# The last norm on three engines, the last convolution's sums in PSUM, and two reordered steps in a two-layer decoder trunk

## The chip, the cores and the metric

The kernel runs on one core of a Trainium2 chip. The metric is the device time of one execution in microseconds. Before the change it is 2335.38 us, the median of 3 runs (2333.52 to 2335.58).

## The reference

A residual stream x of 1024 tokens and 1024 features goes through two layers and a last RMSNorm. All is float32.

```python
for l in range(2):
    h = rmsnorm(x, g_mix[l])
    mem_k, mem_v = split(rmsnorm(mem, g_mem) @ w_mem_kv[l])
    if l == 0:                                # layer A
        p = h @ w_in_a                        # [GLU input 2*768 | memory queries 256]
        v = a * sigmoid(gate)                 # a, gate: the halves of the GLU input
        mix = silu(layernorm(causal_dwconv(v, width 31)))
    else:                                     # layer B
        kvf = rmsnorm(x, g_kv) @ w_kvf        # K, V (12 heads of 64) and 12 forget logits
        cum_logf = cumsum(log_sigmoid(f_logit + b_f))
        q, q_mem = split(h @ w_in_b)
        mix = causal softmax(q k / 8 + cum_logf[t] - cum_logf[s]) @ v
    x = x + concat(mix, memory_attention(q_mem, mem_k, mem_v)) @ w_out[l]
    x = x + conv_ffn(rmsnorm(x, g_ffn[l]))    # up to 2*2816, width-3 conv, silu(gate)*val, down
return rmsnorm(x, g_final)
```

## The kernel before

The stream is kept transposed, features on the 128 partitions and tokens along the free axis: `x[k]` is one of 8 tiles of 128x1024. A float32 product is made of three products of rounded halves (`mm3`, lines 108 to 110): each operand is split into a high and a low part (`split`, lines 81 and 82: ScalarE casts, GpSimd or VectorE subtracts). Tokens are handled in halves of 512 (`hf`).

A planner sets the order on each engine: it takes the instructions in the order in which the code issues them as priorities, estimates when each is ready and how long it takes, and writes one fixed order for each engine, with the semaphores. A tile that takes a slot (its `tag`) waits until the tile before it in that slot has been used for the last time. Three things push the order by hand. `later(100)` lowers the priority of what is issued in it. `issue_after(ins)` puts what it issues behind `ins`, on the engine of `ins` alone. `set_fill` takes a list of small steps, and each `mark` of a matrix product issues the next few of them, so that PE has products to do while an attention waits on other engines; `drain_fill(n)` issues the next n at once.

PSUM has the slots c0 to c3 (128x512 each) and b2a, b2b (128x1024 each). Tiles that ask for "b1" take c0 to c3, or what `ring` names, in turn.

Layer A. Each of the six channel tiles t gets its gate and value products (`ug`, `ua`, in c0 and c1), and then the convolution of 31 taps, split over three engines: PE (`tap`, sums in `cpe`, a b2 slot), GpSimd (ScalarE multiplies into `ct`, GpSimd adds to `yp`, line 875), and VectorE. For t under 5, VectorE adds its taps in place in the PSUM tile `cpe` (line 918). For the last, t = 5, it keeps a sum of its own, `ca`, one 128x512 tile a half, for 10 taps (lines 886 and 888), adds it to `yp` (889), and `rest` adds PE's part and writes `v` (914). PE's taps of t = 5 go half by half. Between these stand the memory attention's steps (scores `ms` in c2, weights `amp`, transposes `mt` in c3, outputs `mo` in c2). Then `lnorm(hf)` sums the six `v` over the channels into `mean`, a tile in c0 for the first half and c1 for the second (line 1014), beside the fill of `mem_step` products (`om`).

Layer B. `normed` puts its sums `st` and broadcasts `bc` in c2 and c3 in turn. `memattn(0)` makes the memory queries `pq` in c0 and c1, and runs the memory attention, with scores in b2 and `mt`, `mo` in c2, c3; its marks issue the V steps. `v_steps(pc_)` makes, for a third of the heads, eight tiles `vps` (one for each 128 tokens, 24 products in four steps), in c0 and c1 in turn; ScalarE and VectorE evict each (lines 1128 to 1131). Then K and Q of the first pair of heads are made (`kq_steps(0)`, 32 steps: K first half, K second half, Q first half, Q second half, 8 steps each; evicted by lines 1181 and 1183). The forget logits become log sigmoids, are transposed (`lft`) and summed along the tokens by one scan on VectorE, `cum` (line 1215). Its high and low parts and their negatives are written to `d_c` and read back as rows of the operands `q2` and `k2` by `prep` (lines 1241 and 1242); the scores of the forgetting attention (1260, 1261, 1263) need them in their second product. Before `prep`, `drain_fill(AHEAD)` with AHEAD = 20 issues 20 steps of the second pair's K and Q; their products take c0, so each half waits until the half before it has been evicted.

The end. `down_final` makes the last down-projection in quarters i of 256 tokens. For each feature tile m: three times three products, VectorE adds to x (662), ScalarE squares (693), GpSimd or, late, VectorE sums the squares (696). Then a square root, a reciprocal (142) and a broadcast row in PSUM, `rows[i]` (123), and `scale(i, k)` multiplies x[k] by `g_final` and the row on VectorE (683) and stores it from SP's queue (685). Those products run FLAG = 15 steps behind; the last fifteen of the 32 come after everything else on VectorE, behind `add2`.

Of the kernel before, what the change touches and what calls it, by code (L numbers as in the profile page):

```python
# [8 lines left out]
F32 = mybir.dt.float32  # L9
F32R = mybir.dt.float32r  # L10
BF16 = mybir.dt.bfloat16
AF = mybir.ActivationFunctionType
ALU = mybir.AluOpType
AX = mybir.AxisListType

P = 128
S = 1024
HS = 512
# [12 lines left out]
VP = 260  # L31
# [20 lines left out]
class Trunk:  # L52
# [363 lines left out]
    def ffn(self, l):  # L416
        nc, tc = self.nc, self.tc
# [214 lines left out]
        with tc.tile_pool(name=f"dn{l}", bufs=1) as fp:  # L632
            self.ps.n, self.ps.ring = 0, ("c0", "c1", "c2", "c3", "b2a", "b2b")
            gs = {}
            G, N0 = 4, 3

            def prep(c):
                w = self.load_w(self.wdn[l, c], [D], name=f"wd{l}",
                                pools=None if c < N0 else ((fp, "dh", 7), (fp, "dl", 7)))
                g = self.main.tile([P, S], F32, tag="raw", name="g", bufs=self.NRAW)  # L640
                nc.sync.dma_start(g, self.d_g[c])
                hs = []
                for hf in range(2):
                    hi, lo = self.htile("gh"), self.htile("gl")
                    self.split(hi, lo, g[:, hf * HS:(hf + 1) * HS])
                    hs.append((hi, lo))
                gs[c] = (hs, w)

            def add_x(k, hf):
                xs = self.nt("xs")  # L650
                sl = slice(hf * HS, (hf + 1) * HS)
                nc.sync.dma_start(xs, self.d_x[:, k, sl])
                nc.vector.tensor_tensor(self.x[k][:, sl], self.x[k][:, sl], xs, op=ALU.add)

            def down_part(ts, m, hf, q=slice(0, HS), first=False):
                ps = self.ps.tile([P, HS], F32, tag="b1", name="dn")[:, :q.stop - q.start]
                self.mm3(ps, [(wh[:, m * P:(m + 1) * P], wl[:, m * P:(m + 1) * P], hs[hf][0][:, q], hs[hf][1][:, q])
                              for hs, (wh, wl) in ts])
                sl = slice(hf * HS + q.start, hf * HS + q.stop)
                if first:  # L660
                    return nc.scalar.copy(self.x[m][:, sl], ps)
                return nc.vector.tensor_tensor(self.x[m][:, sl], self.x[m][:, sl], ps, op=ALU.add)  # L662


            def down(cs):
                ts = [gs.pop(c) for c in cs]
                for hf in range(2):
                    for m in range(KD):
                        down_part(ts, m, hf, first=cs[0] == 0)
                        if cs[0] == N0:  # L670
                            add_x(m, hf)

            def down_final(cs):

                ts = [gs.pop(c) for c in cs]
                Q = 2 * P
                accs = fp.tile([P, 4, Q], F32, tag="y", name="facc", bufs=2)
                sqs = fp.tile([P, 4, Q], F32, tag="y", name="fsq", bufs=2)
                rows, queue = {}, []

                def scale(i, k):
                    sl = slice(i * Q, (i + 1) * Q)
                    nc.vector.scalar_tensor_tensor(self.x[k][:, sl], self.x[k][:, sl], self.vec("g_final", k), rows[i],
                                                   op0=ALU.mult, op1=ALU.mult)
                    nc.sync.dma_start(self.out[:, k, sl], self.x[k][:, sl])

                for i in range(4):
                    sl = slice(i * Q, (i + 1) * Q)
                    acc = accs[:, i]
                    for m in range(KD):  # L690
                        add = down_part(ts, m, i // 2, slice(i % 2 * Q, (i % 2 + 1) * Q))
                        sq = acc if m == 0 else sqs[:, m % 4]
                        nc.scalar.activation(sq, self.x[m][:, sl], AF.Square)
                        if m > 0:
                            e = nc.vector if i == 3 and m >= self.FDVE else nc.gpsimd
                            add2 = e.tensor_tensor(acc, acc, sq, op=ALU.add)
                        g = 8 * i + m - self.FLAG
                        if g >= 0 and g // KD < i:
                            with self.issue_after(add.ins):
                                scale(g // KD, g % KD)  # L700
                            queue.remove((g // KD, g % KD))
                    tmp = self.ps.tile([P, 2, HS], F32, tag="b2", name="fin")
                    r = self.rstd_cols(acc, 2, D, self.eps_rms, tmp[:, 1, :2])
                    rows[i] = self.bcast_row(r, 2, tmp[:, 0, :Q])
                    queue += [(i, k) for k in range(KD)]
                with self.issue_after(add2.ins):
                    for q in queue:
                        scale(*q)

            cs = [list(range(0, N0))] + [list(range(c, min(c + G, NF))) for c in range(N0, NF, G)]  # L710
            for c in cs[0]:
                prep(c)
            self.x = [unit(f"x{k}") for k in range(KD)]
            for i, c in enumerate(cs):
                for c2 in cs[i + 1] if i + 1 < len(cs) else ():
                    prep(c2)
                if i + 1 == len(cs):
                    self.ps.n, self.ps.ring = 0, ("c0", "c1", "c2", "c3")
                (down if l == 0 or i + 1 < len(cs) else down_final)(c)

    def layer_a(self):
        nc, tc = self.nc, self.tc
# [130 lines left out]
        def conv_steps(t):  # L853
# [6 lines left out]
            d = {}  # L860


            def start():
                d["vh"] = pb.tile([P, CW - 1 + S], F32R, tag="vh", name="vh")
                d["vl"] = pb.tile([P, CW - 1 + S], F32R, tag="vl", name="vl")
                self.split(d["vh"], d["vl"], v, lo_eng=nc.vector)
                with self.later(self.LATER):
                    y = d["y"] = pb.tile([P, 2, HS], F32, tag="yp", name="yp", bufs=2)
                    for hf in range(2):
                        nc.scalar.activation(y[:, hf], v[:, hf * HS + ne:hf * HS + ne + HS], AF.Identity,  # L870
                                             bias=self.vec("b_dwa", t), scale=w(ne))
                        for j in range(ne + 1, np_):
                            c = pb.tile([P, HS], F32, tag="ct", name="ct", bufs=2)
                            nc.scalar.activation(c, v[:, hf * HS + j:hf * HS + j + HS], AF.Copy, scale=w(j))  # L874
                            nc.gpsimd.tensor_tensor(y[:, hf], y[:, hf], c, op=ALU.add)  # L875
                if last:

                    with self.later(self.LATER):
                        d["a"] = []
                        for hf in range(2):  # L880
                            a = self.nt("ca")
                            d["a"].append(a)
                            for j in range(np_, CW):
                                vj = v[:, hf * HS + j:hf * HS + j + HS]
                                if j == np_:
                                    nc.vector.tensor_scalar(a, vj, w(j), None, op0=ALU.mult)
                                else:
                                    nc.vector.scalar_tensor_tensor(a, vj, w(j), a, op0=ALU.mult, op1=ALU.add)
                            nc.vector.tensor_tensor(y[:, hf], y[:, hf], a, op=ALU.add)
# [155 lines left out]
    def layer_b(self):  # L1045
# [60 lines left out]
        def v_steps(pc_):  # L1106
# [3 lines left out]
            def step(i):  # L1110
# [2 lines left out]
                if i == 0:  # L1113
                    load_v(pc_ + 1)
                if kk == 0:
                    d["ps"] = self.ps.tile([P, VP], F32, tag=f"c{t % 2}", name="vps")
                ps = d["ps"]
                tsl = slice(ti * P, (ti + 1) * P)
                for k in (2 * kk, 2 * kk + 1):
# [45 lines left out]
        def kq_steps(t):  # L1165
# [3 lines left out]
            def step(i):  # L1169
# [8 lines left out]
                proj_half(d["w" + n], d["u"], hf, [k])  # L1178
                if k == KD - 1:
                    if n == "k":  # L1180
                        nc.vector.tensor_tensor(d[n][:, sl], d["u"], rb[:, sl], op=ALU.mult)
                    else:
                        nc.vector.scalar_tensor_tensor(d[n][:, sl], d["u"], SCALE, rb[:, sl],
                                                       op0=ALU.mult, op1=ALU.mult)
# [27 lines left out]
        on = unit([NFOX, S], F32, "on")  # L1212
        nc.gpsimd.memset(on, 1.0)
        cum = unit([NFOX, S], F32, "cum")
        nc.vector.tensor_tensor_scan(cum, on, lf, 0.0, op0=ALU.mult, op1=ALU.add)
        ch = unit([NFOX, S], F32R, "ch")
        cl = unit([NFOX, S], F32R, "cl")
        nc.scalar.copy(ch, cum)
# [86 lines left out]
                    nc.tensor.matmul(po, lhsT=vs[:, j], rhs=pl[:, u], start=False, stop=j == 2 * I + 1)  # L1305
            self.fold_rows(o, po, e, self.nt("fr", 2 * P))

        self.drain_fill(self.AHEAD)
        vss = {(0, 0): prep(0, 0), (0, 1): prep(0, 1)}
        its = [(t, e, I) for t in range(CT) for e in range(2) for I in range(4)]  # L1310
        pend = []
# [268 lines left out]
```

## Time and profile before

| | |
|---|---|
| median of 3 runs | 2335.38 us (2333.52 to 2335.58) |
| the profiled execution | 2334.59 us |
| its span | 2332.8 us |
| mean granted TensorE clock | 0.988 |
| PE busy | 2256.2 us, 97% |
| VectorE (DVE) busy | 1460.0 us, 63% |
| GpSimd (POOL) busy | 1333.7 us, 57% |
| ScalarE (ACT) busy | 1075.5 us, 46% |
| DMA | 216.74 MB, mean 93 GB/s |

The profile is of one execution on the chip. "PEld" is TensorE's weight load, which overlaps PE's products; "SPq" is the queue from which DMAs are issued. Rows in time give start and length in us, engine, line, operation, output and inputs, shape, how many were merged (x), and in brackets the engine's idle time before and what ended it. Rows of groups give, behind the count, busy us and mean ns of one, then idle us before. Rows of the waits give the total, the number and the longest, in us.

### The profile page before, as it was taken

The page shows a single profiled execution, that of the slowest core. Times are in us where ns is not written, and L with a number is a line of the kernel's source. Part 1 is how long each engine was busy: PE and PEld are TensorE (multiplying, and loading weights), DVE is VectorE, ACT ScalarE, POOL GpSimd, SP SyncE. Part 2 cuts the span into 40 slices and gives each one's busy share as a digit, 9 for nine tenths or more (in the row PEclk, how much of TensorE's full clock was granted, in tenths as well). Part 3 has the DMA queues.
Part 4 walks back from the last instruction along what each step waited for, and adds up shares of the span by engine and source line. Part 5 has one row for each costly group of instructions (what it writes and reads, how often), then busy time and mean ns, then how long its engine had stood idle before and what let it go on. Part 6 is the DMA issues. An engine that isn't in the chain of part 4 may idle for free.

```text
span 2332.8 us, 29689 instructions
## 1 busy us (share of the span) xinstructions
PE 2256.2 (97%) x10970; PEld 1865.7 (80%) x10970; DVE 1460.0 (63%) x1995; ACT 1075.5 (46%) x1864; POOL 1333.7 (57%) x1003
## 2 busy tenths in 40 slices
PE   6999889999999999999998999999999999999998
PEld 6777668878788878888897888788878888778887
DVE  7479787676666664325656777876776666645225
ACT  6776746443434343223542666755444343442212
POOL 3676844666868676453323443614577777766533
PEclk8999989999999999999999999999999999999999
DMA  6100023222222235332332222433222222245322
GB/s 242 37 28 28 29 73 117 72 81 82 82 76 88 78 108 188 106 109 95 123 105 81 71 77 68 124 110 127 67 86 75 81 75 88 79 136 175 112 68 73
DMA packets 85282, 216.74 MB, mean 93 GB/s; under 512 B 9009, under 2 KB 29233, under 8 KB 85137
## 3 DMA queue, kind: packets, MB, share of 16 engines
q1 hardware_dynamic: 84992, 214.52, 28.8%
q8 instruction: 86, 1.41, 0.3%
q14 instruction: 60, 0.48, 0.1%
q10 hardware_dynamic: 144, 0.32, 0.0%
HBM read 156.94 MB, written 51.58 MB: 89 GB/s over the span
## 4 chain that ended last, share of the span: by engine, by line
PE 46%; DVE 3%; POOL 1%; ACT 1%; issue 1%; DMA 0%; DVEq 0%; ACTq 0%; POOLq 0%
PE uY L345 8%; PE uX L345 5%; PE uV L345 5%; PE dn L109 3%; PE dn L108 3%; PE dn L110 3%; PE vps L1122 3%; PE pq L108 2%; PE pq L110 2%; PE pq L109 2%; PE op L108 1%; PE op L109 1%; PE op L110 1%; PE fo L1305 1%; PE fs L1260 1%; PE fo L1304 1%
## 5 line engine op out<-in xcount | busy, mean ns | idle before, releaser
L345 PE MATMUL uY<-fT,fwh 128*128 128x512 f32 x1056 | 331.4, 395 | 4.7 <-DVE fuv L546 3.2
L109 PE MATMUL dn<-gl,wd_hi 128*128 128x512 f32 (+1 forms) x752 | 284.6, 379 | 1.2 <-POOL gl L82 1.2
L108 PE MATMUL dn<-gh,wd_hi 128*128 128x512 f32 (+1 forms) x752 | 280.3, 377 | 0.0
L662 DVE TENSOR_TENSOR fx<-fx,dn 128x512 f32<-128x512 f32 (+1 forms) x176 | 110.9, 636 | 268.8 <-PE dn L110 268.5
L110 PE MATMUL dn<-gh,wd_lo 128*128 128x512 f32 (+1 forms) x752 | 278.9, 375 | 0.0
L345 PEld LDWEIGHTS uY<-fT,fwh 128*128 128x128 f32 x1056 | 196.3, 188 | 55.3 <-DVE fuv L546 9.8
L345 PE MATMUL uX<-fB,fwh 128*128 128x512 f32 x704 | 220.0, 393 | 2.0 <-ACT fuv L521 1.9
L345 PE MATMUL uY<-fT,fwl 128*128 128x512 f32 x528 | 206.6, 391 | 0.0
L82 POOL TENSOR_TENSOR fwl<-wa,fwh 128x512 fp32r<-128x512 f32 x88 | 117.1, 1331 | 137.6 <-ACT fwh L81 137.5
L82 POOL TENSOR_TENSOR wd_lo<-wd_raw,wd_hi 128x1024 fp32r<-128x1024 f32 x44 | 107.9, 2458 | 137.8 <-ACT wd_hi L81 129.0
L108 PEld LDWEIGHTS dn<-gh,wd_hi 128*128 128x128 f32 x752 | 141.2, 188 | 28.3
L109 PEld LDWEIGHTS dn<-gl,wd_hi 128*128 128x128 f32 x752 | 141.3, 188 | 27.0 <-POOL gl L82 2.0
L110 PEld LDWEIGHTS dn<-gh,wd_lo 128*128 128x128 f32 x752 | 141.0, 188 | 27.1
L345 PEld LDWEIGHTS uX<-fB,fwh 128*128 128x128 f32 x704 | 131.6, 188 | 33.3 <-ACT fuv L521 2.8
L82 POOL TENSOR_TENSOR fwl<-wb,fwh 128x512 fp32r<-128x512 f32 x88 | 121.9, 1387 | 63.1 <-ACT fwh L81 60.8
L875 POOL TENSOR_TENSOR yp<-yp,ct 128x512 f32<-128x512 f32 x100 | 135.7, 1359 | 27.6 <-ACT ct L874 22.7
L82 POOL TENSOR_TENSOR gl<-g,gh 128x512 fp32r<-128x512 f32 x88 | 117.5, 1357 | 47.1 <-ACT gh L81 47.1
L345 PE MATMUL uX<-fB,fwl 128*128 128x512 f32 x352 | 137.3, 392 | 0.0
L82 POOL TENSOR_TENSOR fwl<-fs,fwh 128x512 fp32r<-128x512 f32 x88 | 117.8, 1340 | 20.1 <-ACT fwh L81 20.1
L81 ACT CAST fwh<-wa 128x512 fp32r<-128x512 f32 x88 | 54.2, 618 | 140.7 <-PE uY L345 108.3
L81 ACT CAST wd_hi<-wd_raw 128x1024 fp32r<-128x1024 f32 x44 | 45.6, 1050 | 157.6 <-issue 82.2
L345 PEld LDWEIGHTS uY<-fT,fwl 128*128 128x128 f32 x528 | 99.2, 188 | 22.3
(398 smaller groups left out, 6285.4 us busy)
## 6 DMA issues: line engine op xcount, KB each, us to landing
wb<-in_wup SPq DMA_DIRECT2D x44, 512.0 KB
wa<-in_wup SPq DMA_DIRECT2D x44, 512.0 KB
d_g<-fsg SPq DMA_DIRECT2D x44, 512.0 KB
wd_raw<-in_wdn SPq DMA_DIRECT2D x44, 512.0 KB
g<-d_g SPq DMA_DIRECT2D x44, 512.0 KB
d_x<-x SPq DMA_DIRECT2D x32, 256.0 KB
nxs<-d_x SPq DMA_DIRECT2D x32, 256.0 KB
wia_raw<-in_wia SPq DMA_DIRECT2D x14, 512.0 KB
```

The lines of the kernel that those rows point to most:

```text
L81: nc.scalar.copy(hi, src)
L82: (lo_eng or nc.gpsimd).tensor_tensor(lo, src, hi.bitcast(F32), op=ALU.subtract)
L108: nc.tensor.matmul(out, lhsT=ah, rhs=bh, start=start and i == 0, stop=False)
L109: nc.tensor.matmul(out, lhsT=ah, rhs=bl, start=False, stop=False)
L110: nc.tensor.matmul(out, lhsT=al, rhs=bh, start=False, stop=stop and i == n - 1)
L345: mm = nc.tensor.matmul(out, lhsT=w[:, k], rhs=h[k], start=start and k == 0 and j == 0, stop=k == n - 1 and j == 2, skip_group_check=True)
L662: return nc.vector.tensor_tensor(self.x[m][:, sl], self.x[m][:, sl], ps, op=ALU.add)
L875: nc.gpsimd.tensor_tensor(y[:, hf], y[:, hf], c, op=ALU.add)
L1122: nc.tensor.matmul(ps, lhsT=a[hf][k][:, tsl], rhs=w[:, k % 4], start=k == 0 and j == 0, stop=k == KD - 1 and j == 2)
L1260: mm = nc.tensor.matmul(o, lhsT=d["q1"][:, qs], rhs=d["k1"][:, ksl], start=True, stop=False)
L1304: nc.tensor.matmul(po, lhsT=vs[:, j], rhs=ph[:, u], start=j == 0, stop=False)
L1305: nc.tensor.matmul(po, lhsT=vs[:, j], rhs=pl[:, u], start=False, stop=j == 2 * I + 1)
```

## The change

1. `scale`: of the last sixteen products (quarters 2 and 3), six, `shared`, leave VectorE. ScalarE multiplies x by `g_final` right behind the square, ScalarE copies each of the two rows to SBUF (`srows`, in a "raw" slot), and GpSimd multiplies the two.
2. The last convolution's two sums `ca` move from SBUF ("nt" slots) to PSUM, c0 and c1.
3. The first two of the 24 V tiles move from c0 and c1 to c2 and c3.
4. Eight of the twenty steps ahead (K, first half, of the second pair) are issued before the scan, and the scan is put behind the last K eviction issued, which is theirs.

```diff
+                shared = ((2, 1), (2, 3), (2, 5), (2, 7), (3, 0), (3, 1))
+                srows = self.main.tile([P, S], F32, tag="raw", name="frow", bufs=self.NRAW)[:, :2 * Q].rearrange(
+                    "p (i q) -> p i q", i=2)
                 def scale(i, k):
                     sl = slice(i * Q, (i + 1) * Q)
-                    nc.vector.scalar_tensor_tensor(self.x[k][:, sl], self.x[k][:, sl], self.vec("g_final", k), rows[i],
-                                                   op0=ALU.mult, op1=ALU.mult)
+                    if (i, k) in shared:
+                        nc.gpsimd.tensor_tensor(self.x[k][:, sl], self.x[k][:, sl], srows[:, i % 2], op=ALU.mult)
+                    else:
+                        nc.vector.scalar_tensor_tensor(self.x[k][:, sl], self.x[k][:, sl], self.vec("g_final", k),
+                                                       rows[i], op0=ALU.mult, op1=ALU.mult)
                     nc.sync.dma_start(self.out[:, k, sl], self.x[k][:, sl])
...
+                        if (i, m) in shared:
+                            nc.scalar.activation(self.x[m][:, sl], self.x[m][:, sl], AF.Copy,
+                                                 scale=self.vec("g_final", m))
...
                     rows[i] = self.bcast_row(r, 2, tmp[:, 0, :Q])
+                    if i >= 2:
+                        nc.scalar.copy(srows[:, i % 2], rows[i])
...
-                            a = self.nt("ca")
+                            a = self.ps.tile([P, HS], F32, tag=f"c{hf}", name="ca")
...
-                    d["ps"] = self.ps.tile([P, VP], F32, tag=f"c{t % 2}", name="vps")
+                    d["ps"] = self.ps.tile([P, VP], F32, tag=f"c{t % 2 + 2 * (t < 2 and pc_ == 0)}", name="vps")
...
-                        nc.vector.tensor_tensor(d[n][:, sl], d["u"], rb[:, sl], op=ALU.mult)
+                        self.last_k = nc.vector.tensor_tensor(d[n][:, sl], d["u"], rb[:, sl], op=ALU.mult)
...
-        nc.vector.tensor_tensor_scan(cum, on, lf, 0.0, op0=ALU.mult, op1=ALU.add)
+        self.drain_fill(8)
+        with self.issue_after(self.last_k.ins):
+            nc.vector.tensor_tensor_scan(cum, on, lf, 0.0, op0=ALU.mult, op1=ALU.add)
...
-        self.drain_fill(self.AHEAD)
+        self.drain_fill(self.AHEAD - 8)
```

## The prediction

> **What bounds the kernel now.** First the page's slices, for where TensorE (PE) idles; then its longest waits.
>
> ```profile
> PE   6999889999999999999998999999999999999998
> ...
> PE pq L108 <- DVE bkc L1181: 6.9, 2, 6.4
> PE cpe L108 <- DVE v L914: 6.3, 1, 6.3
> ...
> PE vps L1122 <- DVE bmq L247: 0.6, 1, 0.6
> ```
>
> The reader is to see that PE is nearly full, and that the edits stand at holes in it: behind the last convolution (L914), at the start of layer B (L247, and L142 below), and at the running sum (L1181). Behind each hole PE is full, so there a microsecond of PE time saved is one off the end:
>
> ```profile
> 320.00:440.00 120.00, 120.00 (x566) 99.39 (x565) 90.39 (x125) 69.40 (x112) 46.17 (x31) 0.98 0.24 78
> 1130.00:1250.00 120.00, 119.62 (x838) 111.16 (x837) 65.71 (x125) 49.27 (x117) 35.41 (x42) 1.00 0.36 106
> ```
>
> (Length, then busy time of PE, weight loads, VectorE, ScalarE and GpSimd.) The sum is made against the profiled execution, 2334.59 us, 0.8 below the median 2335.38.
>
> **Edit 1, the last convolution's accumulators in PSUM.** The stretch 263 to 325, VectorE by groups, then rows in time:
>
> ```profile
> L888 DVE SCALAR_TENSOR_TENSOR nca<-v,vecs,nca 128x512 f32<-128x512 f32 x18 | 19.6, 1091 | 0.2
> L886 DVE TENSOR_SCALAR nca<-v,vecs 128x512 f32<-128x512 f32 x2 | 2.9, 1456 | 0.1
> ...
> L889 DVE TENSOR_TENSOR yp<-yp,nca 128x512 f32<-128x512 f32 x2 | 2.7, 1370 | 0.0
> ...
> L958 DVE SCALAR_TENSOR_TENSOR v<-ua,vecs,sg 128x512 f32<-128x512 f32 x2 | 1.5, 748 | 1.6 <-PE ua L110 1.6
> ...
> 269.70 3.60 POOL L230 TENSOR_SCALAR amp<-amp,r 128x256 f32<-128x256 f32 x4 [1.52 <-DVE r L267]
> ...
> 308.63 2.27 POOL L230 TENSOR_SCALAR amp<-amp,r 128x256 f32<-128x256 f32 x4 [0.78 <-ACT ct L874]
> ...
> 270.17 3.59 PE L1014 MATMUL mean<-v,inv_conv 128*128 128x512 f32 x8
> ...
> 287.52 5.40 PE L1014 MATMUL mean<-v,inv_conv 128*128 128x512 f32 x8 [2.09 <-DVE v L958]
> ...
> 305.92 0.67 DVE L914 TENSOR_TENSOR v<-yp,cpe 128x512 f32<-128x512 f32 x1
> ...
> 306.65 0.80 PE L108 MATMUL cpe<-vh,dg 128*128 128x512 f32 x1 [6.30 <-DVE v L914]
> ...
> 311.94 0.73 PE L276 MATMUL mt<-ident,amp 128*128 128x128 f32 x4
> ```
>
> L888 reads both operands from SBUF, and takes 1091 ns in the mean; L958, of the same kind and size with one operand in PSUM, takes 748. GpSimd stretches too: four L230 take 3.60 beside a row of L888 and 2.27 elsewhere. So I price all 22 operations at 0.75: 18 x 0.34 + 2 x 0.71 + 2 x 0.62 = 8.8 us less on VectorE. Bounds: nothing, if L958's price doesn't carry over, and 8.8 plus the 1.33 that L230 shows for GpSimd.
>
> [...]
>
> What PE gets: it stands 6.30 us before 306.65, until L914 has run; L914 is behind 13 of the 18 L888, both L886 and one L889, 13 x 0.34 + 1.42 + 0.62 = 6.5 us of the saving, and I add 0.5 for GpSimd, whose sum y L914 also needs. L914, and PE's restart, come 7.0 earlier. From 306.65 to 311.94 PE then gets through 12 products, 0.44 each, where the first window above has 566 instructions in 120.00, 0.21 each: behind the hole it runs at half pace, and 12 x 0.21 from 5.29 leaves 2.7 lost, less some 0.2, as those 566 hold small ones too; I take half of 2.5 back, 1.2.
>
> What it costs: `ca` takes c0 and c1, where the means of lnorm lie. The two rows of L1014 are such sums, eight passes each, that ran ahead in PE's idle time. Now they wait until L889 has freed c0 and c1, and the second half's comes due where PE is full. 16 passes at 3.59/8 = 0.45 are 7.2 us that come back. Between none (they find the rest of the hole) and 9.0 (both rows as they stand) I take 7.2, as the pace of the undisturbed row. Edit 1: -7.0 - 1.2 + 7.2 = -1.0. Ends: -8.2, and +14.0, if VectorE gains nothing, both rows come back and the idle time that they leave, near 270 and before 294, brings two half-pace stretches of 2.5 like the one above. The three nt buffers that it frees hide nothing on PE's path.
>
> **Edit 2, two V tiles to c2 and c3.**
>
> ```profile
> 1115.24 1.05 PE L123 MATMUL bc<-ident,rs 128*128 128x128 f32 x8
> ...
> 1120.69 1.68 PE L123 MATMUL bc<-ident,rs 128*128 128x128 f32 x8 [3.62 <-DVE rs L142]
> ...
> 1118.26 0.27 ACT L140 ACTIVATE sd<-st,eps_rms 128x4 f32<-128x4 f32 x1
> ...
> L1128 ACT ACTIVATE vo<-vps,rs 128x256 fp32r<-128x256 f32 x24 | 11.4, 474 | 20.3 <-PE vps L1122 17.0 <-ACT bmp L265 1.7 <-issue 1.6
> ```
>
> Tiles 0 and 1 no longer wait until the queries leave c0 and c1. c2 holds normed's `st` until the square root has read it, at 1118.53; from there to 1120.69 PE can take 2.1 us of tile 0 (six steps come free with the first two marks). The 0.6 of L247 goes too, since c3 is free earlier. The broadcast behind the hole takes 1.68 against 1.05, and the scores behind it are slow alike: about 1.4 for the low clock, of which I take half. Edit 2: -2.1 - 0.6 - 0.7 = -3.4. Ends: -4.1, and +0.5, if the memory attention's `mt` and `mo`, now behind these tiles in c2 and c3, wait for an eviction (474 ns).
>
> [...]
>
> **Edit 3, the running sum behind a K eviction.** The chain of waits, then rows in time:
>
> ```profile
> 1256.98 3.69 DVE bcum L1215
> 1260.69 1.05 ACT bch L1218
> 1261.76 1.66 DVE bcl L1219
> 1263.42 0.61 DVE bkc L1181
> ...
> 1257.26 0.39 PE L1260 MATMUL fs<-k,q 128*128 128x256 f32 x2
> ...
> 1271.45 0.28 PE L1261 MATMUL fs<-k,q 68*128 68x256 f32 x1
> ...
> 1276.65 0.33 PE L1260 MATMUL fs<-k,q 128*128 128x384 f32 x1
> ...
> 1273.85 0.37 ACT L1271 ACTIVATE ps<-fs,nm 128x128 f32<-128x128 f32 x1
> ...
> 1263.45 0.29 SPq L1221 DMA_DIRECT2D d_c<-bcl  x1
> ...
> 1265.37 0.54 SPq L1241 DMA_DIRECT2D q<-d_c  x2
> 1266.42 0.54 SPq L1242 DMA_DIRECT2D k<-d_c  x2
> ```
>
> PE's next K products need c0, which L1181 empties; L1181 has its input by 1257.5 and stands until 1263.42 behind the scan and bcl. Put first, L1181 ends near 1258.2, and PE goes on 5.8 us earlier. The cost: the scan starts 1.3 later, and behind it wait bch, bcl, the negations, four writes to d_c and four reads on SP's queue, and the scores' second product. A write takes 1.9 (L1221 to L1241), so the reads land near 1268.9 now and 1270.2 then: L1261 moves from 1271.45 only to 1270.2. PE has 36 to 42 products before that, 10 us, and then stands. The third score needs the PSUM of the first, which the exponential (ended 1274.2) frees; it would run near 1273.4 against 1276.65, with as many Q products done. Edit 3: -3.3. Ends: -5.8 - 1.7 (the low clock behind the hole) = -7.5, if the scores' start is covered, and +1.3, if it alone counts. That eight of the twenty steps stand ahead of the scan moves no work.
>
> **Edit 4, the last norm.**
>
> ```profile
> 2315.24 0.73 POOL L696 TENSOR_TENSOR facc<-facc,fsq 128x256 f32<-128x256 f32 x1 [0.38 <-ACT fsq L693]
> ...
> 2321.94 2.82 DVE L683 SCALAR_TENSOR_TENSOR fx<-fx,vecs,fin 128x256 f32<-128x256 f32 x7
> 2324.69 0.16 DVE L142 RECIPROCAL rs<-sd 128x2 f32<-128x2 f32 x1
> 2326.16 3.22 DVE L683 SCALAR_TENSOR_TENSOR fx<-fx,vecs,fin 128x256 f32<-128x256 f32 x8 [1.31 <-PE fin L123]
> ...
> 2322.79 0.26 ACT L140 ACTIVATE sd<-fin,eps_rms 128x2 f32<-128x2 f32 x1 [1.51 <-PE fin L133]
> ...
> 2326.66 0.33 SPq L685 DMA_DIRECT2D out_y<-fx  x1
> ...
> 2330.02 0.40 SPq L685 DMA_DIRECT2D out_y<-fx  x1
> ```
>
> The last reciprocal could run at 2323.05 and stands behind seven products. Four of them go to GpSimd (four of 0.73, free since 2317), three stay, 1.2 us: reciprocal at 2323.2, 1.5 earlier, and the broadcast with it. From there SP's queue sets the end, eight issues 0.48 apart (2326.66 to 2330.02), so the two products taken from the last eight save nothing; their cover is that queue, and if SP holds them first it waits for ScalarE's copy and GpSimd's product, 0.8. ScalarE's six scalings and two copies lie in its idle time. Edit 4: -1.5, ends -1.6 and -0.7.
>
> **Sum.** -1.0 - 3.4 - 3.3 - 1.5 = -9.2: 2325.4 for the profiled execution, 2326.2 against the median.
>
> **The rivals.**
> *More goes:* the sums find the rest of the hole (edit 1 at -8.2) and edit 3 reaches -5.8; -8.2 - 3.4 - 5.8 - 1.5 = -18.9: 2316.5. For it, PE's hole is as long as the sums; against, the scores hang on d_c.
> *Hidden anyway:* the mask rows set the scores' start (-1.2), the V tile isn't put into the hole (-0.6), edit 1 comes out even, edit 4 gives -0.7: 2332.9. For it, L1261's move of 1.2, and that the order of each engine is planned anew, by costs that the trace doesn't show.
> *Slower:* edit 1 loses the early sums and gains nothing on VectorE, its upper end, +14.0, with the other three at -8.2: +5.8, 2341.2. It decides from a price of 12.9 on. Against it, the 1091 ns beside GpSimd. [...]
>
> **How the numbers follow.** Chances: the forecast 0.51 (own range 2321 to 2331), more 0.17, hidden 0.23, slower 0.09. Predicted 2326.2. The range 2315 to 2335 reaches past the rival above and the hidden case and leaves out the slower one and some tails. A difference under 0.2% (4.7 us, so 2330.7 to 2340.1) is about what can't be told from none. Faster: the forecast's and the larger gain's cases, a little of the forecast over the edge, 0.68; same 0.24; slower 0.08.
>
> **What would show each step.** L888's successor near 0.75 us and the hole before the last taps under 2 us, with L1014 in one block late: edit 1 as told; L1014 crowding the stretch behind 310: the slower case. V products between 1118.5 and 1120.7 in place of a hole: edit 2. L1181 ahead of the scan, PE's hole under 1 us there but a new one of 1 to 3 us before the first L1261: edit 3. The last reciprocal within 0.3 us of its square root, and SP's eight issues 1.5 earlier: edit 4. The forecast is wrong if a planned order elsewhere moves by more than these microseconds.

## The result and the profile after

The changed kernel takes 2315.28 us, the median of 4 runs (2313.89 to 2315.91), against 2334.45 us for the kernel before (4 runs): a ratio of 0.9917, with a 95% interval of 0.99 to 0.9935, or 19.2 us less. The forecast was 2326.2, in a range of 2315 to 2335. The time lies only 0.3 above that range's lower end. What came true is the rival "more goes" (2316.5); the sum itself gave 9.2 less, under half of what came.

In the last two groups of experiments the kernel before itself spread over 22.7 and 20.2 us (2333.2 to 2355.9, 2339.2 to 2359.3), so there the profiles' stretches decide more than the medians.

The profiled execution has a span of 2313.2 us (2332.8 before). The page's slices of PE, and then the waits of PE for other engines in the same run (total, times, longest):

```profile
PE   6999899999999999999999999999999999999998
```

```profile
PE fin L133 <- DVE facc L704: 2.6, 1, 2.6
PE cpe L108 <- ACT vh L81: 2.6, 1, 2.6
PE cpe L109 <- DVE vl L82: 2.2, 1, 2.2
```

Of the two long waits of before, the 6.3 for the first addition (now L927) is gone from the list, and the 6.9 for the K eviction has become 1.4 (two waits, the longest 0.9). Between the fifth slice and the last none falls under 9. The first wait of those above is edit 4's; the other two stand in the last convolution, just ahead of where the 6.3 was.

Where the 19.6 us of span came from, by landmarks in both traces: up to `amo` near 255 nothing (0.9 later); from there to the FFN's first product `uX` 10.2 (173.2 to 163.0); from there to the scan 2.4; from the scan to the second layer's `uX` 6.8; in the rest, edit 4's stretch with it, 1.0. The scan stands behind one more eviction and so starts 1.3 later against what is before it (scan alone, below); with that the V tiles' part of the third stretch is 3.7 and the scan's edit 5.5.

Edit 1's stretch after the change, VectorE by groups, then rows in time:

```profile
L901 DVE SCALAR_TENSOR_TENSOR ca<-v,vecs,ca 128x512 f32<-128x512 f32 x18 | 13.5, 748 | 0.2
L899 DVE TENSOR_SCALAR ca<-v,vecs 128x512 f32<-128x512 f32 x2 | 1.5, 750 | 0.0
L902 DVE TENSOR_TENSOR yp<-yp,ca 128x512 f32<-128x512 f32 x2 | 1.4, 681 | 0.3 <-POOL yp L888 0.3
```

```profile
269.29 1.85 POOL L230 TENSOR_SCALAR amp<-amp,r 128x256 f32<-128x256 f32 x4
...
272.47 0.69 DVE L279 TENSOR_TENSOR mtl<-mt,mth 128x512 fp32r<-128x512 f32 x1 [0.29 <-ACT mth L278]
...
296.04 0.67 DVE L927 TENSOR_TENSOR v<-yp,cpe 128x512 f32<-128x512 f32 x1
...
294.90 3.60 PE L1027 MATMUL mean<-v,inv_conv 128*128 128x512 f32 x8
310.29 1.88 PE L1027 MATMUL mean<-v,inv_conv 128*128 128x512 f32 x4
313.39 5.31 PE L1027 MATMUL mean<-v,inv_conv 128*128 128x512 f32 x12
```

And a row of the kernel before that the forecast passed over:

```profile
279.17 0.69 DVE L279 TENSOR_TENSOR mtl<-mt,mth 128x512 fp32r<-128x512 f32 x1 [3.64 <-ACT mth L278]
```

The 22 operations took 25.2 us and take 16.4, and L230 takes 1.85 where it took 3.60. VectorE had stood 3.64 us for `mth`, a copy on ScalarE; now it stands 0.29. Two things changed ahead of that copy: GpSimd's operations became shorter, and the sums `mean` no longer stand in front of the transposes `mt` that it copies (the experiments tell the two apart in part). The addition comes 9.9 earlier. The sums `mean` all run late: eight in what was PE's hole, sixteen behind 310.

Edit 2, PE's rows, and the window with PE's busy time and granted clock (0.94 in the same window before, with 25.62 busy):

```profile
1109.36 0.39 PE L1135 MATMUL vps<-wv_hi,bh 128*128 128x260 f32 x1 [1.50 <-ACT sd L140]
...
1112.34 1.05 PE L123 MATMUL bc<-ident,rs 128*128 128x128 f32 x8
```

```profile
1100.00:1130.00 30.00, 27.42 (x193) 24.80 (x192) 20.81 (x33) 18.03 (x45) 13.80 (x13) 1.00 0.39 127
```

The V tile starts when the square root has left c2, 24 products stand where the hole was, and the broadcast behind takes 1.05 in place of 1.68.

Edit 4, VectorE's and GpSimd's last rows:

```profile
2302.48 1.68 DVE L704 TENSOR_TENSOR facc<-facc,fsq 128x256 f32<-128x256 f32 x2
2304.08 1.25 DVE L691 SCALAR_TENSOR_TENSOR fx<-fx,vecs,fin 128x256 f32<-128x256 f32 x3
2305.26 0.15 DVE L142 RECIPROCAL rs<-sd 128x2 f32<-128x2 f32 x1
2306.62 2.44 DVE L691 SCALAR_TENSOR_TENSOR fx<-fx,vecs,fin 128x256 f32<-128x256 f32 x6 [1.21 <-ACT frow L717]
...
2300.90 2.98 POOL L689 TENSOR_TENSOR fx<-fx,frow 128x256 f32<-128x256 f32 x4 [2.47 <-ACT frow L717]
```

The reciprocal stands right behind its square root, as told. But the two last additions took 1.68 where they took 0.94, beside GpSimd's four products, and the six last products waited for ScalarE's copy.

### The profile page after: what moved, and what is told of

Same layout as the page of the kernel before. It is cut to its first block, busy times and chain, and to the rows that moved or that the text cites. A ratio compares the mean times of both kernels' runs of the same rounds, so it can differ in the third digit from the quotient of the medians.

```text
span 2313.2 us, 29696 instructions
## 1 busy us (share of the span) xinstructions
PE 2249.8 (97%) x10970; PEld 1860.1 (80%) x10970; DVE 1447.1 (63%) x1989; ACT 1078.8 (47%) x1872; POOL 1336.5 (58%) x1009
## 4 chain that ended last, share of the span: by engine, by line
PE 86%; DVE 5%; ACT 3%; DMA 2%; issue 2%; POOL 1%; SPq 0%; DVEq 0%; ACTq 0%; POOLq 0%
PE uY L345 15%; PE uX L345 10%; PE uV L345 10%; PE dn L109 7%; PE dn L108 7%; PE dn L110 7%; PE vps L1135 3%; PE op L108 2%; PE op L109 2%; PE op L110 2%; PE pq L108 2%; PE pq L110 2%; PE pq L109 2%; PE fo L1321 1%; PE ua L108 1%
## 5 line engine op out<-in xcount | busy, mean ns | idle before, releaser
L888 POOL TENSOR_TENSOR yp<-yp,ct 128x512 f32<-128x512 f32 x100 | 131.9, 1322 | 25.8 <-ACT ct L887 20.7
```

## The experiments

**Each edit alone on the kernel before** (the edits are those of the change, one at a time).

> The kernel before with edit 1 alone (the last convolution's accumulators in c0 and c1). Theory A, that the gain seen between 255 and the convolution's last taps is this edit's own: om's last product comes 9 to 10 us earlier than before, and the time falls by 9 (to about 2325.4). The forecast's term says 1.0 less (2333.4). Rival B, that the milestones mix in something of the other edits (the V tiles or the scan shift which stretch runs at the low clock): between those two, 4 to 6 less. In the trace: the addition L914's row near 296 as in the kernel after; mth's copy on ScalarE done by 272, not 278; the first half's eight passes of mean inside the hole, the second half's behind 305.

> The kernel before with edit 2 alone (V tiles 0 and 1 to c2 and c3). Both the forecast's term and the split by milestones say 3.4 to 3.5 less: 2331.0. Rival, that the hole only moves (the square root's release of c2 is as late as that of c0 for what comes next, or the planned order gives the gain back): 0 to 1 less. In the trace: V products from the moment the square root of normed has read c2, and no stretch of half clock behind.

> The kernel before with edit 3 alone (the running sum behind a K eviction, eight of the twenty steps of fill ahead of it). Theory A: 5.8 less (2328.6), because the third score is moved by more than the DMA round trip allows for: the exponential's table is loaded ahead of its first use once Q products run without a gap, so the third score comes 6 to 7 us earlier relative to the scan. The forecast's term says 3.3 less (2331.1). Rival B, that 2 us or more of those 5.8 came from how the stretch lay after edits 1 and 2: 3 to 4 less here. In the trace: the second product of the scores comes 1 to 3 us earlier, the third 6 or more.

> The kernel before with edit 4 alone (six of the last sixteen products shared). Split by milestones: 1.0 less (2333.4). The forecast's term: 1.5 less (2332.9). Rival: no difference, 0 to 0.4 less, if DVE's two additions beside GpSimd's four products and the wait for ScalarE's copy of the last row take it back. In the trace: two additions of facc on VectorE near 0.8 each beside GpSimd's products, and VectorE's last six products waiting 1.0 to 1.3 for ScalarE's copy.

| edit | forecast's term | alone: ratio, 95% interval | in us |
|---|---|---|---|
| 1 PSUM sums | -1.0 | 0.9958 (0.9946 to 0.997) | -9.8 |
| 2 V tiles | -3.4 | 0.9985 (0.9976 to 0.9994) | -3.5 |
| 3 scan | -3.3 | 0.9974 (0.9965 to 0.9983) | -6.1 |
| 4 last norm | -1.5 | 1.0006 (0.9998 to 1.0015) | +1.4 |

The sum is -18.0, against -19.2 for all four together: the edits add up, and no interplay is needed. Edits 1 and 3 carry what the forecast missed; edit 4 gives nothing that can be measured.

**GpSimd's additions left out** (kernel before).

```diff
-                            nc.gpsimd.tensor_tensor(y[:, hf], y[:, hf], c, op=ALU.add)
+                            if not last:
+                                nc.gpsimd.tensor_tensor(y[:, hf], y[:, hf], c, op=ALU.add)
```

> The kernel before, with GpSimd's additions to yp left out in the last convolution (that part of the sum is left out of the output). It tells why an operation on VectorE with both operands in SBUF took 1091 ns. Theory: GpSimd at work on SBUF beside it; then L888's rows fall to 0.75 us without any PSUM, as far as GpSimd is idle then, and the time falls by 6 or more. Rival: the operands' place alone sets it (two SBUF operands are slow with no company): L888 stays near 1.09 us, and only the wait for yp goes.

The ratio is 0.9978 (0.9959 to 0.9997). VectorE's rows and GpSimd's, in time; L889 here is L888 of before, with both operands in SBUF:

```profile
270.59 5.97 DVE L889 SCALAR_TENSOR_TENSOR nca<-v,vecs,nca 128x512 f32<-128x512 f32 x6
...
288.88 0.52 DVE L887 TENSOR_SCALAR nca<-v,vecs 128x512 f32<-128x512 f32 x1
...
299.42 0.74 DVE L889 SCALAR_TENSOR_TENSOR nca<-v,vecs,nca 128x512 f32<-128x512 f32 x1
...
270.74 3.60 POOL L230 TENSOR_SCALAR amp<-amp,r 128x256 f32<-128x256 f32 x4 [1.52 <-DVE r L267]
```

With GpSimd idle (292.8 to 302.8) the operation takes 0.74 to 0.75 us out of SBUF, what it takes out of PSUM in the changed kernel (L901 above, 748 ns in the mean). Six in a row, beside L230 and then beside two additions of GpSimd, take 1.0 each in the mean. Out of PSUM the same company does not show: in the changed kernel GpSimd works beside each of the 18 L901 for 0.89 of its length or more, and each takes 0.74 to 0.76. So for this operation the price went with GpSimd's company when both operands lay in SBUF, and not when one lay in PSUM. GpSimd was not idle altogether in this run (42.5 us of the 117 from 255 to 372), and so all 18 still average 0.90. L887, with one tensor operand and that one in SBUF, is stretched as well: 1.46 on the average before, 0.52 in the row above, with GpSimd idle for the second half of it. Both engines are longer in this company: six of 0.74 and four of 0.46 (L230 in the changed kernel) became 1.0 and 0.90 each; what makes them so is not shown. For this form PSUM was not dearer, 0.75 against 0.74. The form with one tensor input did become dearer, 0.52 (L887) against 0.75 (L899 of the changed kernel), in one operation here; what makes it so is not shown.

The run shows another thing about edit 1. The first addition comes 7.6 earlier after `amo` than before, but VectorE still stands for `mth`:

```profile
280.80 0.69 DVE L279 TENSOR_TENSOR mtl<-mt,mth 128x512 fp32r<-128x512 f32 x1 [2.54 <-ACT mth L278]
```

So without GpSimd's additions this wait shrinks from 3.64 only to 2.54; their company is not all of it.

**The sums late, the accumulators still in SBUF** (kernel before).

```diff
                             nc.vector.tensor_tensor(y[:, hf], y[:, hf], a, op=ALU.add)
+                            hold = self.ps.tile([P, HS], F32, tag=f"c{hf}", name="hold")
+                            nc.vector.tensor_copy(hold[:, :1], a[:, :1])
```

> The kernel before (accumulators in SBUF), with a PSUM tile in c0 and c1 that holds one column of each finished accumulator, so that the sums of mean come as late as with edit 1, while the 22 operations keep their operands. It prices the forecast's step of 16 passes, 7.2 us, by itself. Forecast's step: 7 more (2341.5). Rival: half of them find PE's hole before the last taps, which stays as long as before (about 6), and only the second half's eight passes come back: 3.6 more (2338). A third: nothing that is measured (the hole behind the second sums, or before 294, only moves). If edit 1's gain came from the order of the sums and not from the operations' price, this would be faster than before.

The ratio is 1.0018 (1.0003 to 1.0034): slower, so the order of the sums alone does not gain. From `amo` to `uX` it takes 176.1 us against 173.2, although its first addition came 2.5 earlier (the planned order moved too). The price of the late sums is then 2.9 to 5.4 here, where I had 7.2; the interval of the times, 0.7 to 8.0, holds both. It is not a clean price: the 22 operations took 21.3 in place of 25.2 here, with the same operands; the planned order, and with it what stands beside them, had moved. And VectorE's wait for `mth` is nearly gone, though the accumulators are in SBUF and the four transposes `mt` still stand for L230, its results 0.88 apart:

```profile
274.69 0.69 DVE L279 TENSOR_TENSOR mtl<-mt,mth 128x512 fp32r<-128x512 f32 x1 [0.50 <-ACT mth L278]
```

With the sums out of the way PE makes `mt` sooner. The 2.5 of this run and the 7.6 of the run without GpSimd's additions come near the 10.3 by which the first addition is earlier after `amo` with edit 1 alone.

**The first half's accumulator alone in PSUM** (kernel before).

```diff
-                            a = self.nt("ca")
+                            a = self.ps.tile([P, HS], F32, tag="c0", name="ca") if hf == 0 else self.nt("ca")
```

> The kernel before with the first half's accumulator alone in PSUM (c0); the second half's stays in SBUF, and its eight passes of mean can run early again. If the operations' price on the way to the first addition L914 is what counts (the first half's chain), this keeps nearly all of edit 1's 9.8 and may add the 3.6 of the second half's passes: 10 to 13 less, 2322. Rival: the second half's operations, which lie between on the same engine, still take 1.09 us each, L914 comes some 3 us later than with both, and the gain is 5 to 8. Third: the second half's early passes take PE's time ahead of the first addition anyway, no difference from both (9.8).

The ratio is 0.9968 (0.995 to 0.9986), 7.5 less, with 7.7 less between `amo` and `uX`: the first rival's 5 to 8. VectorE's groups:

```profile
L888 DVE SCALAR_TENSOR_TENSOR nca<-v,vecs,nca 128x512 f32<-128x512 f32 x9 | 9.3, 1037 | 0.0
L888 DVE SCALAR_TENSOR_TENSOR ca<-v,vecs,ca 128x512 f32<-128x512 f32 x9 | 6.8, 753 | 0.2
```

In one run the half that moved takes 753 ns, and the one that stayed 1037.

**Edit 3's drain without the order to wait** (kernel before): `drain_fill(8)` ahead of the scan, `drain_fill(self.AHEAD - 8)` later, and no `issue_after`.

> The kernel before with edit 3's first half alone: eight of the twenty steps of fill are drained ahead of the running sum, and no order to issue the scan behind the last K eviction. Theory: the order on VectorE decides, so the K eviction still stands behind the scan and bcl, PE's hole of 6 stays, and the time is that of before (2334.4, give or take 1). Rival: the planner puts the eviction first by itself once the steps are ahead: 5 to 6 less, as with the whole edit.

The ratio is 0.9963 (0.9943 to 0.9982): the rival was right, and my theory fell. VectorE's rows here, and then the rows of VectorE, ScalarE and PE in the run with the whole of edit 3 alone:

```profile
1258.43 0.69 DVE L1181 TENSOR_TENSOR bkc<-pq,rb 128x512 f32<-128x512 f32 x1 [0.57 <-PE pq L110]
1259.04 2.60 DVE L1216 TENSOR_TENSOR_SCAN bcum<-bon,blf 12x1024 f32<-12x1024 f32 x1
```

```profile
1257.97 2.60 DVE L1217 TENSOR_TENSOR_SCAN bcum<-bon,blf 12x1024 f32<-12x1024 f32 x1
...
1265.45 1.28 ACT L1273 ACT_TABLE_LOAD   x1
...
1268.92 0.28 PE L1263 MATMUL fs<-k,q 68*128 68x256 f32 x1
...
1270.15 0.44 PE L1262 MATMUL fs<-k,q 128*128 128x384 f32 x1 [0.63 <-ACT ps L1273]
```

The planner (the part of the program that sets the order of the operations) puts the eviction first by itself once its steps stand ahead; the explicit order adds nothing that shows.

**The changed kernel, and three versions of it, on one chip.** Without edit 4; with four products shared in place of six, and no copy for the last quarter (`shared` cut to its first four, `if i == 2:`); and without edit 4 but with the split of the last `v` in halves:

```diff
-                self.split(d["vh"], d["vl"], v, lo_eng=nc.vector)
+                for sl in (slice(0, HS + CW - 1), slice(HS + CW - 1, None)) if last else (slice(None),):
+                    self.split(d["vh"][:, sl], d["vl"][:, sl], v[:, sl], lo_eng=nc.vector)
```

> The changed kernel once more, on the chip on which the next three run, so that they can be held against it within a microsecond or so: 19 less than before (ratio near 0.992).

> The changed kernel without edit 4 (the last norm as before; edits 1 to 3 in place). Each edit alone gave 9.8, 3.8, 6.0 and 0.0 less than before. Theory: edit 4 gives nothing in company either, so this stands within 0.5 of the changed kernel. Rival, by the split by milestones and the forecast: edit 4 is worth 1.0 to 1.5 once the rest is in, and this is slower than the changed kernel by that. In the trace the last reciprocal stands 1.6 behind its square root again, but the last eight products start 1.3 behind it with no copy in front.

> The changed kernel with only four products shared, those of the third quarter; the last quarter's eight stay on VectorE and ScalarE's copy of its row goes. Theory: VectorE's last products waited for that copy (0.37) after the broadcast, though they read PSUM and not the copy; without it they start 0.4 earlier, and as SP's eight issues set the end, the time falls by 0.4, at most 0.7 against the changed kernel. Rival: the copy cost nothing, and two products more on VectorE cost up to 0.8: 0 to 0.8 slower.

> As the run without edit 4, and in addition the last convolution's split of v into vh and vl is made in two halves (543 and 511 columns) in place of one of 1054. In the changed kernel PE stood 2.55 us for vh and 2.17 for vl at the first product of the last taps, with a stretch of low clock behind; the first taps need the first half alone. Theory, that the stretch is still bound by this hole: 3 to 5 less than the run without edit 4, and the low stretch behind 282 goes or is shorter. Rival: PE's hole only moves to before the first addition's taps (VectorE is full from 285 to 305), and nothing or under 1 is gained.

The ratios to the kernel before are 0.9882 (0.9852 to 0.9912), 0.9901 (0.9864 to 0.9939), 0.9893 (0.9868 to 0.9918) and 0.9881 (0.9854 to 0.9908). By times none can be told from another, and no version is shown to beat the changed kernel. The profiles tell more. For the norm, from the start of the last two additions to the span's end: 11.72 us before, 11.77 without edit 4, 11.31 with edit 4 alone, 10.72 and 11.60 in two profiles of the changed kernel, 11.04 with four shared. Edit 4 is worth 0.1 to 1.0 there. The two profiles of the changed kernel differ by PE's pace behind the same wait of 2.59: the sums `fin` took 0.58 in one and 0.96 in the other, the broadcast 0.71 and 1.23. VectorE's last row with four shared:

```profile
2315.19 3.22 DVE L691 SCALAR_TENSOR_TENSOR fx<-fx,vecs,fin 128x256 f32<-128x256 f32 x8 [1.32 <-PE fin L123]
```

Without the copy the last products stand 1.32 for the broadcast; with edit 4 alone, where the broadcast took as long (1.22 and 1.23), they stood 1.72, for the copy. They read PSUM and not the copy; whether it is the planned order or two readers of one tile that holds them was not tried.

For the halves, PE's waits from 255 to 372, and VectorE (the third busy time) in two of its windows:

```profile
PE ms L259 <- ACT amp L265: 3.3, 1, 3.3
PE mean L1015 <- DVE yp L890: 3.0, 1, 3.0
```

```profile
285.00:295.00 10.00, 3.72 (x10) 2.24 (x10) 10.00 (x14) 6.21 (x15) 9.61 (x9) 0.69 0.86 320
295.00:305.00 10.00, 10.00 (x32) 6.04 (x32) 10.00 (x12) 4.95 (x8) 9.53 (x11) 0.80 0.02 6
```

Both waits for `vh` and `vl` are gone, and two of 3.3 and 3.0 stand instead, just behind. From `amo` to `uX` it took 162.7 us against 162.9 without the halves. The rival was right: VectorE is full from 285 to 305, and until its accumulators are done PE's hole can only move.

## Why the prediction was right or wrong

It helps to count what PE loses over a whole stretch, its idle time and what the low clock takes, rather than hole by hole. From 255 to 372, before, after, the late sums and GpSimd's additions left out, each from its own trace:

```profile
255.00:372.00 117.00, 104.04 (x466) 80.90 (x465) 88.02 (x107) 70.43 (x123) 69.90 (x53) 0.93 0.16 54
```

```profile
255.00:372.00 117.00, 111.33 (x512) 88.31 (x511) 84.34 (x114) 75.64 (x131) 69.84 (x58) 0.94 0.19 67
```

```profile
255.00:372.00 117.00, 102.54 (x454) 80.21 (x453) 87.97 (x109) 71.63 (x123) 76.00 (x57) 0.90 0.17 58
```

```profile
255.00:372.00 117.00, 108.40 (x496) 85.14 (x495) 86.59 (x111) 71.55 (x126) 42.50 (x33) 0.96 0.19 64
```

Idle time (117 less PE's busy time) and 117 times the clock that is missing add up to 21.2 us before, 12.7 after, 26.2 and 13.3. That the missing clock costs PE its share of the time is an estimate, from the products for K in the kernel before: 0.43 apart at a granted clock of 0.50 (1265 to 1267), 0.23 apart at 1.00 (from 1268 on). Against before that is -8.5, +5.0 and -7.9, where the stretch from `amo` to `uX` moved by -10.2, +2.9 and -6.7. The clock has two digits, and a second profile of the changed kernel gives 10.8 in place of 12.7, so each sum is good to about two microseconds; the order and the rough sizes hold.

*Edit 1, forecast -1.0, measured -9.8.* The price of the operations was right: 8.8 us off VectorE was forecast, and 25.2 - 16.4 = 8.8 came. Two terms failed. The first is "I add 0.5 for GpSimd": VectorE no longer stands for `mth` (3.64 to 0.29), so the addition came 9.9 earlier where 7.0 was forecast. That GpSimd's company is what made VectorE's operations long, the run without GpSimd's additions shows (L889 0.74 to 0.75 where GpSimd was idle, 1.0 in the six beside it). For the wait it is only a part: 2.54 was left there, while the late sums with the accumulators in SBUF left 0.50. So the sums' move, with the order planned around it, which I had down as a cost alone, also lets `mth` come early. How the two share the gain is read from these traces (7.6 and 2.5), not tried in one run. The second is "16 passes ... come back", +7.2. They came back, but PE's products are the same as before; here the moved work cost only the idle time that it left behind, and the earlier VectorE filled that with other products. Idle time fell by 7.3. I had added the passes at full price on top of a hole that they partly fill: that is the rival's "the sums find the rest of the hole".

*Edit 2, forecast -3.4, measured -3.5 (-5.6 to -1.4).* The step held: start at the square root, 1.5 us of hole left. The low clock behind went altogether, where I had taken half: the window's clock is 1.00 with this hole of 1.50, where it was 0.94 with the one of 3.62. A hole shorter than 3.62 did not leave the clock at 1.00 every time: the last section shows a wait of 2.55 in which it fell to 0.50.

*Edit 3, forecast -3.3, measured -6.1.* The step that failed is "L1261 moves from 1271.45 only to 1270.2", and the third score "near 1273.4". With edit 3 alone they came at 1268.92 and 1270.15. The scan started 1.0 later by the span's clock (1.3 against the FFN before it), as told, but took 2.60 in place of 3.69 and so ended no later. In the traces GpSimd's subtraction for `q`, which ends near 1258.5, lies beside the first 1.5 us of the longer one and the first 0.5 of the shorter; no run took that away alone. And a piece was not in the sum at all, in the kernel before:

```profile
1271.48 1.05 ACT L81 CAST wq_hi<-wq_raw 128x1024 fp32r<-128x1024 f32 x1 [6.91 <-PE pq L109]
1272.55 1.28 ACT L1271 ACT_TABLE_LOAD   x1
```

ScalarE's table load stood behind a cast that waited 6.91 for PE's products. With PE going on it starts at 1265.45 and is done by 1266.73, ahead of the scores, and the third score waits only 0.63. Of the 3.3 by which the third score came before its forecast (1270.15 against 1273.4), 1.3 is L1261 (1268.92 against 1270.2), and 2.0 is that the score followed it after 1.2 and not 3.2. In the kernel before L1261 had no wait in front of it: it stood behind products for K in PE's order, so it was not `d_c`'s readers that held it. The new hole of 1 to 3 us that I expected before L1261 did not appear. "That eight of the twenty steps stand ahead of the scan moves no work" was wrong too: it alone makes the gain.

*Edit 4, forecast -1.5, measured none (+1.4, interval -0.5 to +3.5).* The reciprocal moved as told. Not priced were the additions beside GpSimd, 0.74 longer (the same company as in edit 1, which I had just read off L888 and did not carry over), and the copy ahead of the last products, 0.4.

*The cases.* The forecast's own range began at 2321, and the chance of 0.17 for "more goes" was too low. Its mechanism for edit 1 was right; its -5.8 for edit 3 was right in size. That the stated range of 2315 to 2335 still holds the time, by 0.3, is owed to its width and so to luck: two of the four terms, edits 1 and 3, were too small by 8.8 and 2.8, and edit 4's 1.5 did not come. "Slower" fell with GpSimd's price, which held in full.

## What to carry to other kernels

Count PE's idle time and low clock over the whole stretch; work that is moved cost here only the idle time that it left, not its length (sixteen passes of 0.45 us came back, and idle time fell by 7.3). Before an operation is priced, see who works beside it: here a VectorE operation with two SBUF operands took 0.74 to 1.76 us with GpSimd at work beside it (1.09 in the mean of the 18 L888) and 0.74 to 0.75 without it, and GpSimd's L230 took 0.90 in place of 0.46 for each tile. One operand in PSUM was enough to end that on both engines: 0.75 and 0.46, beside each other. When a hole goes, ask what else on the other engines was waiting for PE.

## What the runs showed of the hardware that was not expected

Waits of PE between 2.1 and 2.6 us came out either way for its clock. In the changed kernel PE stood 2.55 from 279.95, and the granted clock went from 1.00 to 0.50 at about 282, within that wait; it stayed there until 292.2, past the next wait of 2.17. Score products right behind the first wait took 0.41 in place of 0.28:

```profile
282.50 0.79 PE L108 MATMUL cpe<-vh,dg 128*128 128x512 f32 x1 [2.55 <-ACT vh L81]
283.09 0.41 PE L259 MATMUL ms<-aks,amq 128*128 128x256 f32 x1
...
286.31 0.80 PE L109 MATMUL cpe<-vl,dg 128*128 128x512 f32 x1 [2.17 <-DVE vl L82]
```

In the kernel before a wait of 2.17, up to 279.19, left the clock at 1.00, and one of 2.09, up to 287.52, was followed by 0.50 from 288.3. In the last norm the wait of 2.59, up to 2304.31, left it at 1.00 until 2306.0, and 0.50 came just behind; in the other profile of the changed kernel the sums behind that wait took 0.96 in place of 0.58. The lone hole of 1.50 near 1108 left the clock at 1.00. What decides between them is not shown here.

In three of the profiles (the drain without the order, four shared, the halves) PE stood 5.7 to 5.8 us at one product `uY` of an FFN, for VectorE's `fuv`, and with four shared and the halves the way from `uX` to the scan was 8.4 to 8.7 us longer than without edit 4 on the same chip. No edit touches that stretch. With four shared the trace shows what stood ahead of that `fuv` on VectorE: one multiplication, L547, with both operands in SBUF, took 7.96 us. Its median in the kernel before is 1.29 and its longest there 1.84. A short one and the long one, with four shared:

```profile
717.10 0.69 DVE L547 TENSOR_TENSOR fuv<-fuv,rb 128x512 f32<-128x512 f32 x1
...
736.52 7.96 DVE L547 TENSOR_TENSOR fuv<-fuv,rb 128x512 f32<-128x512 f32 x1
```

In the kernel before, the four of its 44 rows with GpSimd idle beside them took 0.68 each, and the forty with GpSimd at work beside some or all of their length 0.68 to 1.84, 1.32 in the mean. So the company that edit 1 ended in the convolution is still there in the FFN. What stood beside the row of 7.96, and why PE stood like this in some executions only, is not shown here.
